# Weight buffers at eight offsets from a multiple of 512 bytes, and each unit's matmuls sorted by width

## The chip, the core and the metric

The kernel runs on one core of a Trainium2 chip. The metric is the device time of one execution in microseconds (us), the median of three runs. TensorE multiplies matrices, VectorE (DVE in the profile) and ScalarE (ACT) work elementwise, GpSimd is POOL, and SyncE (SP) issues most DMAs. A matmul on TensorE has two operands in the on-chip memory SBUF: the stationary one (128 columns of 128 partitions here), which is loaded into the array by an instruction of its own (PEld, LDWEIGHTS in the profile), and the moving one, which is streamed through, up to 512 columns. The result is added up in PSUM.

## What is computed

A decoder trunk of two layers on 256 tokens of width 2048, in float32. Cut to what matters:

```python
for l in range(2):
    h = rms_norm(x, norm_mix[l])
    p = h @ w_in[l]                        # (256, 2048) @ (2048, 6656)
    x = x + mixers(p) @ w_out[l]           # three kinds of attention; (256, 2048) @ (2048, 2048)
    u = rms_norm(x, norm_ffn[l])
    gate = causal_dwconv(u @ w_gate[l])    # (256, 2048) @ (2048, 5504)
    x = x + (silu(gate) * (u @ w_up[l])) @ w_down[l]    # (256, 5504) @ (5504, 2048)
return rms_norm(x)
```

Nearly all work is in these five products with weights.

## The kernel before

**Precision in two parts.** A float32 number is held as a pair of float32r numbers, hi and lo, where lo is what hi leaves over. The product of two such numbers is made of hi·hi, hi·lo and lo·hi. The operand (h, the mixers' output or the activation) lies in tiles `hp`, `mixp` and `actp`, which hold, for 128 rows of the reduction, 256 tokens of hi and then 256 tokens of lo, so 512 columns. A weight tile comes by DMA as float32 (`raw`, five buffers) and is split: ScalarE copies it into `whi` (line 169, by the helper in line 122), VectorE subtracts into `wlo` (line 170).

**Units.** The weights come in units of 128 x 1024 elements, 788 in all. `dma_unit` loads unit u + 7, `split_unit` splits unit u + 3, and `mm_unit` issues the matmuls of unit u; each is called once per step of one loop over all units. `whi` and `wlo` have four buffers each of 4096 bytes in a partition, used in turn. After the matmuls of a unit the loop lets the mixers' and other elementwise steps go on (`steps.run`).

**Two modes.** In mode B (676 units: the projections that are wanted transposed, the output, gate, up and down products) a slice of 128 weight columns is stationary. For each slice there are two matmuls: line 202 with the `whi` slice as stationary operand and all 512 columns of the operand as moving one (hi·hi and lo·hi side by side), and line 203 with the `wlo` slice and the operand's 256 columns of hi. A unit has eight such pairs. The text calls the matmul of 512 columns H and that of 256 L; before, they alternate H, L, H, L. In mode A (112 units) the operand's slices of 128 tokens are stationary and 512 weight columns move, three matmuls (lines 209, 210 and 211) for each slice, 12 in a unit.

**Accumulators.** Each output block (a chunk) adds up in one of two accumulators, `acc`, each of two PSUM banks. When a chunk has had its last matmul, its results are taken over by ScalarE and VectorE while the next chunk fills the other accumulator. The down product has 43 slices of the reduction for a chunk, four in a unit, so some of its units hold the end of one chunk and the start of the next.

**Addresses.** A slice of weights is 512 bytes long in a partition, and the operands' slices start at multiples of 1024 bytes (mode B) or 512 (mode A) in their tiles. In the program as built all these tiles, `whi`, `wlo`, `hp`, `mixp` and `actp`, start 128 bytes behind a multiple of 512, so every weight load and every moving operand of these matmuls starts at the same remainder of 512 bytes.

**Order of the work.** The order on each engine is the order in which the code issues instructions; the tile framework adds the semaphore waits. The first H of a unit waits for ScalarE's copy, the first L for VectorE's subtraction, ScalarE's copy into a `whi` buffer for the last matmul that read it four units ago.

Of the kernel before, what the change touches and what calls it, by code (L numbers as in the profile page):

```python
# [10 lines left out]
F32 = mybir.dt.float32  # L11
F32R = mybir.dt.float32r
# [4 lines left out]
P = 128  # L17
S = 256
# [64 lines left out]
def hybrid_kernel(ctx: ExitStack, tc: tile.TileContext, io):  # L83
    nc = tc.nc

    wpool = ctx.enter_context(tc.tile_pool(name="wpool", bufs=4))
# [33 lines left out]
    def act(out, in_, fn, **kw):  # L120
        want(fn)
        nc.scalar.activation(out, in_, fn, **kw)  # L122
# [30 lines left out]
    def dma_unit(u, parts=1, between=None):  # L153
# [5 lines left out]
                between()  # L159
        raws[u] = t  # L160

    def split_unit(u, parts=1):
        r = raws.pop(u)
        hi = wpool.tile([P, 1024], F32R, name=f"whi{u}", tag="whi")
        lo = wpool.tile([P, 1024], F32R, name=f"wlo{u}", tag="wlo")
        n = 1024 // parts
        for i in range(parts):
            cs = slice(i * n, (i + 1) * n)
            act(hi[:, cs], r[:, cs], AF.Copy)
            nc.vector.tensor_tensor(lo[:, cs], r[:, cs], hi[:, cs].bitcast(F32), op=OP.subtract)  # L170
        splits[u] = (hi, lo)

    def mm_unit(u, f_only=None):
        hi, lo = splits[u]
        ended = []
        off = 0
        for ch, kt in units[u][1]:
            if ch.begin is not None and not ch.begun:
                ch.begin()
            for _ in range(200):  # L180
                if ch.need(kt) and (ch.acc is not None or ACC.free):
                    break
                steps.run(1e9, 1e9)
            assert ch.need(kt)
            if ch.acc is None:
                ch.acc = ACC.get([P, 1024], F32, f"acc_{u}")
            acc = ch.acc[0]
            first = not ch.begun
            ch.begun = True
            last = ch.left == 1  # L190
            if f_only != 0:
                ch.left -= 1
            if u == nu - 1:
                last = kt == NF - 1
            pair, j = ch.operand(kt)
            x = pair[:, j].rearrange("p a t -> p (a t)")
            if ch.mode == "B":
                for f in range(ch.ncol // P) if f_only is None else (f_only,):
                    w = slice(off + f * P, off + (f + 1) * P)
                    o = acc[:, f * 512:(f + 1) * 512]  # L200

                    nc.tensor.matmul(o, hi[:, w], x, start=first, stop=False, skip_group_check=True)  # L202
                    nc.tensor.matmul(o[:, 0:S], lo[:, w], x[:, 0:S], start=False, stop=last, skip_group_check=True)  # L203
            else:
                w = slice(off, off + 512)
                for t in range(2):
                    xh, xl = x[:, t * P:(t + 1) * P], x[:, S + t * P:S + (t + 1) * P]
                    o = acc[:, t * 512:(t + 1) * 512]
                    nc.tensor.matmul(o, xh, hi[:, w], start=first, stop=False)  # L209
                    nc.tensor.matmul(o, xh, lo[:, w], start=False, stop=False)  # L210
                    nc.tensor.matmul(o, xl, hi[:, w], start=False, stop=last)  # L211
            off += ch.ncol
            if ch.left == 0:
                ended.append(ch)
        return ended


# [139 lines left out]
    part = {}  # L357
# [742 lines left out]
    steps.add(first_stats(), 0)  # L1100
    build_h(0, g0)
    split_unit(0, 2)
    dma_unit(3)
    build_h(1, g0)
    split_unit(1)
    dma_unit(4)
    xin(6)
    xin(7)
    build_h(2, g0)
    build_h(3, g0)  # L1110
    split_unit(2)
    dma_unit(5)
    dma_unit(6)
    for u in range(nu):
        if u in (1, 2):
            build_h(2 * u + 2, g0)
            build_h(2 * u + 3, g0)
        if u + 3 < nu:
            split_unit(u + 3)
        if u + 7 < nu:  # L1120
            dma_unit(u + 7)
        if u == nu - 1:

            mm_unit(u, 0)
            ended = mm_unit(u, 1)
        else:
            ended = mm_unit(u)
        del splits[u]
        steps.run(1.25, 1.3)
        for ch in ended:  # L1130
            if ch.after is not None:
                ch.after()
            ch.done(ch.acc)
            new = steps.live[[x[1] for x in steps.live].index(steps.n - 1)]
            try:
                next(new[2])
            except StopIteration:
                steps.live.remove(new)
# [86 lines left out]
```

## Time and profile before

| | |
|---|---|
| median of 3 runs | 2298.92 us (2298.28 to 2299.11) |
| the profiled execution | 2298.39 us |
| its span, first to last instruction | 2296.5 us |
| TensorE busy, matmuls | 2274.6 us (99%), 12724 instructions |
| weight loads busy | 1978.1 us (86%), 12724 instructions |
| VectorE busy | 1512.8 us (66%) |
| ScalarE busy | 1087.1 us (47%) |
| bytes moved by DMA | 425.10 MB, mean 185 GB/s |

The profile records one execution. A row of its groups gives the line, the engine, the operation, the tiles (output <- inputs), shapes, the count, busy time and the mean duration of one, and the idle time of the engine before these instructions with what ended it. A row of the timeline gives start and duration in us, engine, line and operation. TensorE's matmuls are pipelined: the record of one lasts longer than the distance to the start of the next, and the ends are modelled, so this document takes distances from start to start. A matmul of plain float32 is recorded as two, so there are more records than matmuls.

### The profile page before, as it was taken

The page shows a single profiled execution, that of the slowest core. Times are in us where ns is not written, and L with a number is a line of the kernel's source. Part 1 is how long each engine was busy: PE and PEld are TensorE (multiplying, and loading weights), DVE is VectorE, ACT ScalarE, POOL GpSimd, SP SyncE. Part 2 cuts the span into 40 slices and gives each one's busy share as a digit, 9 for nine tenths or more (in the row PEclk, how much of TensorE's full clock was granted, in tenths as well). Part 3 has the DMA queues.
Part 4 walks back from the last instruction along what each step waited for, and adds up shares of the span by engine and source line. Part 5 has one row for each costly group of instructions (what it writes and reads, how often), then busy time and mean ns, then how long its engine had stood idle before and what let it go on. Part 6 is the DMA issues. An engine that isn't in the chain of part 4 may idle for free.

```text
span 2296.5 us, 32374 instructions
## 1 busy us (share of the span) xinstructions
PE 2274.6 (99%) x12724; PEld 1978.1 (86%) x12724; DVE 1512.8 (66%) x1898; ACT 1087.1 (47%) x1388; POOL 176.9 (8%) x150
## 2 busy tenths in 40 slices
PE   8999999999999999999999999999999999999997
PEld 7788888888888888888888888888888888888886
DVE  5685556777777777555567755577777777765554
ACT  5654544454444444444456454444444444444442
POOL 0150001100000000000012400020000000001111
PEclk9999999999999999999999999999999999999999
DMA  7454454655555555555555445555555555555553
GB/s 264 167 173 168 165 189 167 197 186 193 188 190 191 193 189 187 192 190 188 191 195 181 165 166 173 175 179 198 193 189 187 193 192 186 191 192 188 189 192 110
DMA packets 120580, 425.10 MB, mean 185 GB/s; under 512 B 13515, under 2 KB 17132, under 8 KB 120428
## 3 DMA queue, kind: packets, MB, share of 16 engines
q1 hardware_dynamic: 118412, 420.50, 53.3%
q10 hardware_dynamic: 2016, 2.54, 0.3%
q8 instruction: 100, 1.64, 0.3%
q14 instruction: 52, 0.43, 0.1%
HBM read 419.31 MB, written 3.67 MB: 184 GB/s over the span
## 4 chain that ended last, share of the span: by engine, by line
PE 94%; POOL 2%; issue 1%; DVE 1%; ACT 1%; DMA 0%; DVEq 0%; SPq 0%; ACTq 0%; POOLq 0%
PE acc L202 54%; PE acc L203 28%; PE acc L209 3%; PE acc L211 3%; PE acc L210 3%; POOL hx L488 0%; POOL hx L489 0%; DVE wlo L170 0%; DMA raw<-in_w_b 0%; PE ps_rstd L1096 0%; PE ps_qk L680 0%; PE ps_o L710 0%; ACT whi L122 0%; PE ps_pt L700 0%; PE ps_rs L793 0%
## 5 line engine op out<-in xcount | busy, mean ns | idle before, releaser
L170 DVE TENSOR_TENSOR wlo<-raw,whi 128x1024 fp32r<-128x1024 f32 (+1 forms) x789 | 998.9, 1269 | 728.0 <-ACT whi L122 721.5
L202 PE MATMUL acc<-hp,whi 128*128 128x512 f32 x3520 | 1230.1, 394 | 6.7 <-ACT whi L122 5.8
L122 ACT ACTIVATE whi<-raw 128x1024 fp32r<-128x1024 f32 (+1 forms) x789 | 831.5, 1056 | 809.6 <-PE acc L202 553.5
L203 PE MATMUL acc<-hp,wlo 128*128 128x256 f32 x3520 | 986.1, 280 | 0.0
L202 PEld LDWEIGHTS acc<-hp,whi 128*128 128x128 f32 x3520 | 660.3, 188 | 154.9 <-ACT whi L122 5.8
L203 PEld LDWEIGHTS acc<-hp,wlo 128*128 128x128 f32 x3520 | 666.8, 189 | 0.7 <-DVE wlo L170 0.4
L202 PE MATMUL acc<-actp,whi 128*128 128x512 f32 x1376 | 477.1, 391 | 0.0
L203 PE MATMUL acc<-actp,wlo 128*128 128x256 f32 x1376 | 385.3, 280 | 0.0
L202 PEld LDWEIGHTS acc<-actp,whi 128*128 128x128 f32 x1376 | 257.4, 187 | 56.3
L203 PEld LDWEIGHTS acc<-actp,wlo 128*128 128x128 f32 x1376 | 260.4, 189 | 0.0
L209 PE MATMUL acc<-whi,hp 128*128 128x512 f32 x448 | 181.6, 405 | 0.0
L202 PE MATMUL acc<-mixp,whi 128*128 128x512 f32 x512 | 178.9, 395 | 0.0
L248 POOL TENSOR_TENSOR sq<-xt 128x512 f32<-128x512 f32 x31 | 33.2, 1070 | 1862.1 <-DVE xt L319 1198.7
L211 PE MATMUL acc<-whi,hp 128*128 128x512 f32 x448 | 175.1, 391 | 0.0
L210 PE MATMUL acc<-wlo,hp 128*128 128x512 f32 x448 | 174.6, 390 | 0.0
L203 PE MATMUL acc<-mixp,wlo 128*128 128x256 f32 x512 | 142.0, 277 | 0.0
L202 PEld LDWEIGHTS acc<-mixp,whi 128*128 128x128 f32 x512 | 96.1, 188 | 21.9
L209 PEld LDWEIGHTS acc<-whi,hp 128*128 128x128 f32 x448 | 84.2, 188 | 18.8 <-issue 1.6
L211 PEld LDWEIGHTS acc<-whi,hp 128*128 128x128 f32 x448 | 84.1, 188 | 18.2
L210 PEld LDWEIGHTS acc<-wlo,hp 128*128 128x128 f32 x448 | 84.3, 188 | 16.5
L203 PEld LDWEIGHTS acc<-mixp,wlo 128*128 128x128 f32 x512 | 96.2, 188 | 0.0
L122 ACT ACTIVATE actp<-up 128x512 fp32r<-128x512 f32 (+1 forms) x44 | 27.4, 623 | 83.3 <-DVE up L849 83.3
(196 smaller groups left out, 1189.8 us busy)
## 6 DMA issues: line engine op xcount, KB each, us to landing
raw<-in_w_d SPq DMA_DIRECT2D x172, 512.0 KB, 3.3
raw<-in_w_g SPq DMA_DIRECT2D x168, 512.0 KB, 3.2
raw<-in_w_u SPq DMA_DIRECT2D x168, 512.0 KB, 3.2
raw<-in_w_a SPq DMA_DIRECT2D x112, 512.0 KB, 3.2
raw<-in_w_b SPq DMA_DIRECT2D x95, 512.0 KB, 3.2
raw<-in_w_out SPq DMA_DIRECT2D x64, 512.0 KB, 3.3
xt<-in_x SPq DMA_DIRECT2D x8, 256.0 KB, 6.1
bias<-brow_d SPq DMA_DIRECT2D x4, 512.0 KB, 5.1
```

The lines of the kernel that those rows point to most:

```text
L122: nc.scalar.activation(out, in_, fn, **kw)
L170: nc.vector.tensor_tensor(lo[:, cs], r[:, cs], hi[:, cs].bitcast(F32), op=OP.subtract)
L202: nc.tensor.matmul(o, hi[:, w], x, start=first, stop=False, skip_group_check=True)
L203: nc.tensor.matmul(o[:, 0:S], lo[:, w], x[:, 0:S], start=False, stop=last, skip_group_check=True)
L209: nc.tensor.matmul(o, xh, hi[:, w], start=first, stop=False)
L210: nc.tensor.matmul(o, xh, lo[:, w], start=False, stop=False)
L211: nc.tensor.matmul(o, xl, hi[:, w], start=False, stop=last)
L248: nc.gpsimd.tensor_tensor(sq, x, x, op=OP.mult)
```

## The change

**Pads.** The four rotating buffers of `whi` and `wlo` become eight single buffers, named by the unit number modulo 4, and ahead of each, when it is first made, a small tile is allocated that is never used: 32 bytes ahead of `whi0`, 96 ahead of `wlo0`, 64 ahead of each other one. The buffers then start 32, 128, 192, 256, 320, 384, 448 and 512 bytes further on than the operands do, counted in remainders of 512: in this order `whi0`, `wlo0`, `whi1`, `wlo1`, `whi2`, `wlo2`, `whi3`, `wlo3`. The last of them has the operands' own remainder again. The operand tiles keep theirs. A buffer is still used by every fourth unit.

**Order.** `mm_unit` first collects the pieces of the unit, then issues all H, then all L. Mode A keeps its order.

```diff
+    lead = {"whi0": 32, "wlo0": 96, "whi1": 64, "wlo1": 64, "whi2": 64, "wlo2": 64, "whi3": 64, "wlo3": 64}
+
+    def split_tile(kind, u):
+        tag = f"{kind}{u % 4}"
+        if tag in lead:
+            wpool.tile([P, lead.pop(tag) // 4], F32, name=f"lead_{tag}", tag=f"lead_{tag}", bufs=1)
+        return wpool.tile([P, 1024], F32R, name=f"{kind}{u}", tag=tag, bufs=1)
...
-        hi = wpool.tile([P, 1024], F32R, name=f"whi{u}", tag="whi")
-        lo = wpool.tile([P, 1024], F32R, name=f"wlo{u}", tag="wlo")
+        hi = split_tile("whi", u)
+        lo = split_tile("wlo", u)
...
+            pieces.append((ch, pair[:, j].rearrange("p a t -> p (a t)"), ch.acc[0], off, first, last))
...
+        for part in range(2):
+            for ch, x, acc, off, first, last in pieces:
+                if ch.mode == "A":
+                    continue
                 for f in range(ch.ncol // P) if f_only is None else (f_only,):
                     w = slice(off + f * P, off + (f + 1) * P)
                     o = acc[:, f * 512:(f + 1) * 512]
 
-                    nc.tensor.matmul(o, hi[:, w], x, start=first, stop=False, skip_group_check=True)
-                    nc.tensor.matmul(o[:, 0:S], lo[:, w], x[:, 0:S], start=False, stop=last, skip_group_check=True)
...
+                    if part == 0:
+                        nc.tensor.matmul(o, hi[:, w], x, start=first, stop=False, skip_group_check=True)
+                    else:
+                        nc.tensor.matmul(o[:, 0:S], lo[:, w], x[:, 0:S], start=False, stop=last, skip_group_check=True)
```

TensorE's rows in the gate product of layer 0, unit 160 and the start of unit 161, before (the tiles' numbers tell buffers apart; each H and L shown here stands four times in a row, in turns, and the repeats are left out):

```order
L202 MATMUL acc_160_4406<-hp_3163,whi160_4324 128x512
L203 MATMUL acc_160_4406<-hp_3163,wlo160_4325 128x256
...
L202 MATMUL acc_160_4406<-hp_3196,whi160_4324 128x512
L203 MATMUL acc_160_4406<-hp_3196,wlo160_4325 128x256
...
L202 MATMUL acc_160_4406<-hp_3296,whi161_4347 128x512
L203 MATMUL acc_160_4406<-hp_3296,wlo161_4348 128x256
```

And the same units in the changed kernel:

```order
L221 MATMUL acc_160_4414<-hp_3171,whi160_4332 128x512 x4
L221 MATMUL acc_160_4414<-hp_3204,whi160_4332 128x512 x4
L223 MATMUL acc_160_4414<-hp_3171,wlo160_4333 128x256 x4
L223 MATMUL acc_160_4414<-hp_3204,wlo160_4333 128x256 x4
L221 MATMUL acc_160_4414<-hp_3304,whi161_4355 128x512 x4
L221 MATMUL acc_160_4414<-hp_3404,whi161_4355 128x512 x4
```

Where there were eight changes from 512 to 256 columns in a unit there is one, between its eighth and ninth matmul.

In the down product of layer 0, TensorE's rows where unit 318 holds the end of one chunk and the start of the next, before:

```order
L202 MATMUL acc_308_8054<-actp_8123,whi318_8214 128x512
L203 MATMUL acc_308_8054<-actp_8123,wlo318_8215 128x256
...
L202 MATMUL acc_318_8298<-actp_4077,whi318_8214 128x512
L203 MATMUL acc_318_8298<-actp_4077,wlo318_8215 128x256
...
L202 MATMUL acc_318_8298<-actp_4077,whi319_8236 128x512
```

And after:

```order
L221 MATMUL acc_308_8062<-actp_8131,whi318_8222 128x512 x2
L221 MATMUL acc_318_8294<-actp_4085,whi318_8222 128x512 x2
L223 MATMUL acc_308_8062<-actp_8027,wlo318_8223 128x256 x4
L223 MATMUL acc_308_8062<-actp_8131,wlo318_8223 128x256 x2
L223 MATMUL acc_318_8294<-actp_4085,wlo318_8223 128x256 x2
L221 MATMUL acc_318_8294<-actp_4085,whi319_8244 128x512 x2
```

The old chunk's last L now stands behind the new chunk's first two H.

More of the change, by code (lines that the diff above doesn't have):

```diff
@@ L176, in mm_unit @@
         off = 0
+        pieces = []
         for ch, kt in units[u][1]:
@@ L186, in mm_unit @@
                 ch.acc = ACC.get([P, 1024], F32, f"acc_{u}")
-            acc = ch.acc[0]
             first = not ch.begun
@@ L195, in mm_unit @@
             pair, j = ch.operand(kt)
-            x = pair[:, j].rearrange("p a t -> p (a t)")
-            if ch.mode == "B":
+            pieces.append((ch, pair[:, j].rearrange("p a t -> p (a t)"), ch.acc[0], off, first, last))
+            off += ch.ncol
+            if ch.left == 0:
+                ended.append(ch)
+        for part in range(2):
+            for ch, x, acc, off, first, last in pieces:
+                if ch.mode == "A":
+                    continue
                 for f in range(ch.ncol // P) if f_only is None else (f_only,):
@@ L200, in mm_unit @@
                     o = acc[:, f * 512:(f + 1) * 512]
[L202 to L214, printed above, removed]
+                    if part == 0:
+                        nc.tensor.matmul(o, hi[:, w], x, start=first, stop=False, skip_group_check=True)
+                    else:
+                        nc.tensor.matmul(o[:, 0:S], lo[:, w], x[:, 0:S], start=False, stop=last, skip_group_check=True)
+        for ch, x, acc, off, first, last in pieces:
+            if ch.mode == "B":
+                continue
+            w = slice(off, off + 512)
+            for t in range(2):
+                xh, xl = x[:, t * P:(t + 1) * P], x[:, S + t * P:S + (t + 1) * P]
+                o = acc[:, t * 512:(t + 1) * 512]
+                nc.tensor.matmul(o, xh, hi[:, w], start=first, stop=False)
+                nc.tensor.matmul(o, xh, lo[:, w], start=False, stop=False)
+                nc.tensor.matmul(o, xl, hi[:, w], start=False, stop=last)
         return ended
```

## Prediction

> **What bounds the kernel now.** I read the page first: engine shares, TensorE's clock, then the chain of work that ended last.
>
> ```profile
> span 2296.5 us, 32374 instructions
> PE 2274.6 (99%) x12724; PEld 1978.1 (86%) x12724; DVE 1512.8 (66%) x1898; ACT 1087.1 (47%) x1388; POOL 176.9 (8%) x150
> PEclk9999999999999999999999999999999999999999
> PE 94%; POOL 2%; issue 1%; DVE 1%; ACT 1%; DMA 0%; DVEq 0%; SPq 0%; ACTq 0%; POOLq 0%
> ```
>
> TensorE is busy for 99% of the span at the full granted clock, and 94% of the chain is TensorE. The groups of instructions say which matmuls these are (the last two columns are the idle time before them and its cause).
>
> ```profile
> L202 PE MATMUL acc<-hp,whi 128*128 128x512 f32 x3520 | 1230.1, 394 | 6.7 <-ACT whi L122 5.8
> L202 PE MATMUL acc<-actp,whi 128*128 128x512 f32 x1376 | 477.1, 391 | 0.0
> L202 PE MATMUL acc<-mixp,whi 128*128 128x512 f32 x512 | 178.9, 395 | 0.0
> L209 PE MATMUL acc<-whi,hp 128*128 128x512 f32 x448 | 181.6, 405 | 0.0
> L211 PE MATMUL acc<-whi,hp 128*128 128x512 f32 x448 | 175.1, 391 | 0.0
> L210 PE MATMUL acc<-wlo,hp 128*128 128x512 f32 x448 | 174.6, 390 | 0.0
> L203 PEld LDWEIGHTS acc<-hp,wlo 128*128 128x128 f32 x3520 | 666.8, 189 | 0.7 <-DVE wlo L170 0.4
> ```
>
> So there are 3520 + 1376 + 512 = 5408 pairs of mode B (one matmul of 512 columns, H, and one of 256, L) and 3 x 448 = 1344 matmuls of mode A (512 columns): 12160 in all, each with its own weight load, and almost no idle time. A mean of 394 ns is no price, since neighbours overlap; the price is the distance from start to start. I take it from stretches where nothing else runs on TensorE: from the stages view for mode B in the feed-forward part of layer 0 (first row: window, busy, matmuls in brackets), and from the timeline for mode A, the first and the last start of 48 matmuls (four units of 12).
>
> ```profile
> 500.00:850.00 350.00, 350.00 (x2021) 1.00 0.55 190
> ```
>
> ```profile
> 1184.35 0.39 PE L209 MATMUL acc<-whi,hp 128*128 128x512 f32 x1
> 1195.23 0.39 PE L209 MATMUL acc<-whi,hp 128*128 128x512 f32 x1
> ```
>
> A pair costs 350 us / 1010.5 = 346.4 ns, a matmul of mode A 10.88 us / 48 = 226.7 ns. If a matmul costs r per column and b besides, 512r + b = 226.7 and 768r + 2b = 346.4 give r = 0.42 ns and b = about 13 ns. The streaming cannot be changed by this edit. The 13 ns can, in principle: 12160 x 13 ns = 158 us of the span.
>
> What are these 13 ns? Two places of the timeline tell something. The first is the start of the kernel, where TensorE runs at half its pace (the clock column says 1.00 there too, so the profile doesn't show why):
>
> ```profile
> 7.56 0.63 PE L202 MATMUL acc<-hp,whi 128*128 128x512 f32 x1
> 8.20 0.63 PE L202 MATMUL acc<-hp,whi 128*128 128x512 f32 x1
> ```
>
> A pair takes 640 ns there, which is 768 columns at 0.83 ns, exactly twice r, and nothing besides. So the extra is no fixed toll for each matmul: it appears only when the moving operand is read at full pace, as if the weight load that runs beside it took turns of the same read. The second place is in layer 1, in units of mode B behind a run of mode A; the rows are the start of an H and the start of the next A, seven units or 56 pairs later.
>
> ```profile
> 1200.76 0.40 PE L202 MATMUL acc<-hp,whi 128*128 128x512 f32 x1
> 1220.55 0.40 PE L209 MATMUL acc<-whi,hp 128*128 128x512 f32 x1
> ```
>
> These pairs cost 19.79 us / 56 = 353.4 ns with the same tiles at the same remainders of 512 bytes: 7.0 ns more than in the feed-forward part. So the extra depends on how loads and streams stand to each other in time, and it settles into one of two states.
>
> **The change part by part.** *The pads.* Seven of eight weight buffers get another remainder of 512 bytes against the operand tiles. Their price is not in the trace of before, because there all weights and operands have the same remainder. From both sides: if the remainder shifts loads against streams as favourably as possible, it could take off all of the 13 ns; the nearest row for an unfavourable shift is the 7.0 ns a pair (3.5 ns a matmul) of the state above. I take nothing, because the trace has met several relations in time already (the start of every stage, every interruption by another matmul) and always came back to 346.4 or 353.4 ns, never to less: an offset in address looks to me like another start of the same game. The Trainium skill (SBUF — State Buffer, Who interferes with whom) says that TensorE reads through two independent ports, one for moving data and one for weights, and waits on no engine; by that the pads are worth nothing. The trace doesn't agree on the reason, since a load beside a stream does cost it 13 ns here.
>
> *The order inside a unit.* H and L each keep their count, columns, weight load and accumulator. If every matmul kept its own share, a unit would cost what it did, 8 x 346.4 ns. What is new is that each of the 676 units of mode B (5408 / 8) now has a run of eight H, then a run of eight L, and so two changes of kind. Before, such changes only stand at stage borders. From B to A (the L is followed by 512-column matmuls) the timeline has, for the first A, the one eight later and the one twelve after that:
>
> ```profile
> 320.30 0.39 PE L209 MATMUL acc<-whi,hp 128*128 128x512 f32 x1
> 322.14 0.39 PE L211 MATMUL acc<-whi,hp 128*128 128x512 f32 x1
> 324.86 0.39 PE L211 MATMUL acc<-whi,hp 128*128 128x512 f32 x1
> ```
>
> The first eight take 1.84 us, 27 ns above 8 x 226.7; the next twelve take 2.72 us, 226.7 each. A run of 512-column matmuls behind a 256-column one needs about eight to settle, which is as long as the new run is. From A to B the first pair is:
>
> ```profile
> 1197.95 0.39 PE L202 MATMUL acc<-hp,whi 128*128 128x512 f32 x1
> 1198.29 0.40 PE L202 MATMUL acc<-hp,whi 128*128 128x512 f32 x1
> ```
>
> 340 ns, so some 6 to 7 ns come back there. Net 20 ns for each unit: 676 x 20 ns = 13.5 us. L behind L has no row (no 256-column matmul of this dtype stands behind another); its bounds are the cheapest and dearest shares seen, 0 and 27 ns more for a unit if it needs settling as well, and a gain isn't excluded but I have no row for one. I take 0.
>
> *Waits.* The page's waits, in total, times and longest:
>
> ```profile
> DVE wlo L170 <- ACT whi L122: 721.5, 633, 4.8
> ACT whi L122 <- PE acc L202: 553.5, 329, 2.4
> ACT up L122 <- PE acc L203: 76.8, 42, 1.8
> ```
>
> The hi buffer is now read last in the middle of its unit, so ScalarE's copy may start up to eight L earlier (half of 8 x 346 ns at most); the lo buffer is needed seven H later (7 x 227 ns = 1.6 us). Both only lengthen waits of engines at 66% and 47%. Where a unit of the down projection holds the end of one accumulator and the start of the next, the ended one now waits for up to six more H (1.4 us); the other accumulator is in use for another 43 x 2 pairs (30 us), which covers it. At the start:
>
> ```profile
> 5.82 0.80 PE L202 MATMUL acc<-hp,whi 128*128 128x512 f32 x1 [5.82 <-ACT whi L122]
> 6.54 0.58 PE L203 MATMUL acc<-hp,wlo 128*128 128x256 f32 x1
> ```
>
> The first L follows the first H after 0.72 us, of which some tenths may be spared when other H stand between them. The slow state of the 56 pairs, 0.39 us there, could go as well. All of this I set to 0, with 1 us of gain as the bound.
>
> **The sum.** The profiled execution took 2298.39 us (its span of 2296.5 and 1.9 around it), 0.5 us under the median of the three runs, 2298.92. 2298.4 + 13.5 = 2311.9; with the half us, 2312.
>
> **Rivals.** *Nothing moves* (2299, 2294 to 2303): runs of eight settle into the same 13 ns a matmul, since nearly all stages of before did so whatever came ahead, and the pads do nothing. Against it: the 27 ns at 320 us, which recurs at the other borders.
>
> *The pads keep loads and streams apart (faster).* Place: every weight load beside a full-pace stream. For it: at half pace the cost is nil, so it is a collision, and the 353.4 against 346.4 ns shows that it depends on a relation between the two reads. All 12160 matmuls of before have one relation of addresses, so the trace can't say that another is no better. Price: one step like that between the two states, 3.5 ns for a matmul, on seven buffers of eight: 12160 x 7/8 x 3.5 ns = 37 us, so 2262; all 13 ns would give 2160. It decides from 13.5 us / 12160 = 1.1 ns a matmul upwards, where it outweighs the changes of kind. The Trainium skill (TensorE: Matmul & The Clock Gate, Back-to-back issue gap) gives columns / 2.4 GHz + 2.5 ns for a warm matmul; an estimate from it is 215.8 ns for 512 columns where the trace has 226.7, so by that page some 11 ns of each matmul would be there to win.
>
> *The pads make it worse*: other remainders hold the stream in the dearer state, +3.5 ns on seven of eight: 37 us, 2336. For it: the state exists; against it: only 56 pairs in a row and some shorter pieces were in it.
>
> **How the numbers follow.** Changes of kind cost (the forecast; its own range goes from half the price, 2306, to twice, 2326) 0.34; nothing moves 0.28; faster by the pads 0.29; slower by the pads 0.09. A measurement of this kernel can tell about 0.2%, 4.6 us, from no change. Faster: 0.29 and 0.01 of the case at rest, 0.30; within 0.2%: 0.27; slower: 0.34 + 0.09 = 0.43. The range goes from 2240, which takes in a gain by the pads of one and a half steps (56 us) and leaves out larger ones, some 0.10, to 2336, which leaves out about 0.05.
>
> **What would show it.** In the feed-forward stage after, an H run's distances start above 227 ns and fall, and eight pairs of a unit take 2.79 us instead of 2.77. If distances differ between the four hi buffers (unit number modulo 4), the pads matter; if all H take 227 ns and all L 120 ns, nothing moved. I am wrong if a unit takes 2.77 us or less, or if mode A, whose order is kept, leaves 226.7 ns: that would be the pads alone.

## The result and the profile after

| | before | after |
|---|---|---|
| median, measured side by side | 2298.74 us (4 runs) | 2317.22 us (4 runs, 2317.03 to 2317.41) |
| ratio, 95% interval | | 1.0078 [1.0065, 1.0091] |
| span of the profiled execution | 2296.5 us | 2315.2 us |

The change makes the kernel 18.5 us slower. The forecast was 2312 us, slower, inside a range of 2240 to 2336. The page of the changed kernel, the same four lines that were shown of before:

```profile
span 2315.2 us, 32374 instructions
PE 2294.0 (99%) x12724; PEld 1984.8 (86%) x12724; DVE 1495.9 (65%) x1898; ACT 1084.4 (47%) x1388; POOL 181.3 (8%) x150
PEclk9999999999999999999999999999999999999998
PE 94%; POOL 2%; issue 1%; DVE 1%; ACT 1%; DMA 0%; SPq 0%; DVEq 0%; ACTq 0%; POOLq 0%
```

Counts, clock and chain are as before; TensorE's busy time has grown by 19.4 us, the span by 18.7. So the time was not lost to a wait: the same matmuls cost more. Where, a unit at a time, is read from the timeline. These are the first H of five units in a row in the feed-forward part of layer 0 (start, duration of the whole run of eight), with one run of L between:

```profile
619.58 2.02 PE L221 MATMUL acc<-hp,whi 128*128 128x512 f32 x8
621.43 1.10 PE L223 MATMUL acc<-hp,wlo 128*128 128x256 f32 x8
622.38 2.00 PE L221 MATMUL acc<-hp,whi 128*128 128x512 f32 x8
...
625.16 2.03 PE L221 MATMUL acc<-hp,whi 128*128 128x512 f32 x8
...
627.98 2.00 PE L221 MATMUL acc<-hp,whi 128*128 128x512 f32 x8
...
630.77 0.40 PE L221 MATMUL acc<-hp,whi 128*128 128x512 f32 x1
```

From start to start the four units take 2.80, 2.78, 2.82 and 2.79 us. The same distances over the whole stage, unit number modulo 4 from 0 to 3, are 2796, 2783, 2820 and 2794 ns. Before, every one was 2773; there the starts of two units, four apart, are

```profile
615.51 0.39 PE L202 MATMUL acc<-hp,whi 128*128 128x512 f32 x1
...
626.61 0.39 PE L202 MATMUL acc<-hp,whi 128*128 128x512 f32 x1
```

So units have grown, and the four buffers differ. The second place to look is mode A, whose order is the same. The first matmul of a unit in layer 1, and of the one four units on:

```profile
1190.82 0.39 PE L231 MATMUL acc<-whi,hp 128*128 128x512 f32 x1
...
1201.93 0.39 PE L231 MATMUL acc<-whi,hp 128*128 128x512 f32 x1
```

11.11 us, where it was 10.88: 231.5 ns a matmul instead of 226.7. The order of these matmuls is the same, so this points at the pads; e1, which has the order alone, shows it.

The one wait that the change was to shorten did get shorter: what ScalarE's copy into `whi` waits for TensorE has gone from 553.5 to 461.0 us, since H now come first and let go of the buffer sooner.

```profile
ACT whi L122 <- PE acc L221: 461.0, 284, 1.8
```

It is worth nothing here, since ScalarE is busy for 47% of the span and TensorE doesn't wait for it.

I summed the 787 distances from the start of one unit to the start of the next in each trace and took before's away: mode B +15.3 us, mode A +3.8 us. Two theories stood against each other for these: that the changes of kind cost 13.5 us as forecast and the pads the rest, or that the pads do all or most of it.

### The profile page after: what moved, and what is told of

The parts are those of the page before. It is cut to its first block, busy times and chain, and to the rows that moved or that the text cites. A ratio compares the mean times of both kernels' runs of the same rounds, so it can differ in the third digit from the quotient of the medians.

```text
span 2315.2 us, 32374 instructions
## 1 busy us (share of the span) xinstructions
PE 2294.0 (99%) x12724; PEld 1984.8 (86%) x12724; DVE 1495.9 (65%) x1898; ACT 1084.4 (47%) x1388; POOL 181.3 (8%) x150
## 4 chain that ended last, share of the span: by engine, by line
PE 94%; POOL 2%; issue 1%; DVE 1%; ACT 1%; DMA 0%; SPq 0%; DVEq 0%; ACTq 0%; POOLq 0%
PE acc L221 54%; PE acc L223 28%; PE acc L231 3%; PE acc L232 3%; PE acc L233 3%; POOL hx L507 0%; POOL hx L508 0%; DVE wlo L180 0%; DMA raw<-in_w_b 0%; PE ps_rstd L1115 0%; PE ps_qk L699 0%; PE ps_o L729 0%; ACT whi L122 0%; PE ps_pt L719 0%; PE ps_rs L812 0%
## 5 line engine op out<-in xcount | busy, mean ns | idle before, releaser
L122 ACT ACTIVATE whi<-raw 128x1024 fp32r<-128x1024 f32 (+1 forms) x789 | 830.0, 1056 | 709.3 <-PE acc L221 461.0
L221 PE MATMUL acc<-hp,whi 128*128 128x512 f32 x3520 | 891.5, 395 | 6.2 <-DVE hp L253 6.1
L221 PEld LDWEIGHTS acc<-hp,whi 128*128 128x128 f32 x3520 | 632.5, 189 | 125.2 <-ACT whi L122 6.4
L223 PEld LDWEIGHTS acc<-hp,wlo 128*128 128x128 f32 x3520 | 480.1, 189 | 37.5
L223 PE MATMUL acc<-hp,wlo 128*128 128x256 f32 x3520 | 490.0, 282 | 0.0
L221 PE MATMUL acc<-actp,whi 128*128 128x512 f32 x1376 | 346.2, 393 | 0.0
L223 PEld LDWEIGHTS acc<-actp,wlo 128*128 128x128 f32 x1376 | 187.5, 189 | 14.7
L223 PE MATMUL acc<-actp,wlo 128*128 128x256 f32 x1376 | 191.4, 282 | 0.0
L221 PE MATMUL acc<-mixp,whi 128*128 128x512 f32 x512 | 129.7, 395 | 0.0
L223 PEld LDWEIGHTS acc<-mixp,wlo 128*128 128x128 f32 x512 | 69.7, 189 | 5.5
L122 ACT ACTIVATE hp<-xt,par 128x256 fp32r<-128x256 f32 x64 | 28.7, 500 | 94.6 <-DVE xt L338 93.2
```

## The experiments

A number of bytes below is the offset of a buffer against the operand tiles, counted in remainders of 512, as in the section on the change. "Unit" is the distance from the start of one unit of mode B to the next in the feed-forward part of layer 0, before 2773 ns; its columns alone are 8 x 320 = 2560 ns, by the 640 ns of a pair at half pace. So the extra of a unit of before is 213 ns.

The extra isn't made by the other engines. Near the end of before, in units 785 and 786, all weights are loaded and split, and VectorE, ScalarE and GpSimd are idle and the DMA nearly so (the columns are the window, then busy time and instructions of PE, PEld, DVE, ACT and POOL, the clock, and the DMA's share and rate):

```profile
2272.60:2278.10 5.50, 5.50 (x34) 4.84 (x33) 0.00 (x0) 0.00 (x0) 0.00 (x0) 1.00 0.01 3
```

These two units take 2773 and 2774 ns, like those of the feed-forward stage. So TensorE's own loads and streams are enough to make the extra.

### The two halves of the change

**e1: the order alone.** The buffers stay as they were.

```diff
+        for part in range(2):
+            for ch, x, acc, off, first, last in pieces:
...
+                    if part == 0:
+                        nc.tensor.matmul(o, hi[:, w], x, start=first, stop=False, skip_group_check=True)
+                    else:
+                        nc.tensor.matmul(o[:, 0:S], lo[:, w], x[:, 0:S], start=False, stop=last, skip_group_check=True)
```

> The sorted order without the pads (weight buffers as before, four of each, all at the operands' remainder of 512 bytes). Theory K (the changes of kind cost, as predicted): mode B units take about 2.80 us as in the changed kernel (2774 + 25 ns), mode A units go back to 2720 ns, in all about 2311 us (676 x 25 ns = 16.9 us less what little the order saves elsewhere). Theory P (the pads cost, the order nothing): 2774 ns a unit, 2297 to 2300 us. If both have a part, a unit of mode B lies between 2774 and 2799 ns.

2310.43 us, ratio 1.005 [1.0035, 1.0065], +11.8 us. The timeline's rows of one unit and the start of the unit four later:

```profile
617.89 2.00 PE L213 MATMUL acc<-hp,whi 128*128 128x512 f32 x8
619.74 1.12 PE L215 MATMUL acc<-hp,wlo 128*128 128x256 f32 x8
620.69 2.00 PE L213 MATMUL acc<-hp,whi 128*128 128x512 f32 x8
...
629.07 0.40 PE L213 MATMUL acc<-hp,whi 128*128 128x512 f32 x1
```

Four units take 11.18 us, so 2.795 us each; the median over the stage is 2793 ns, 20 ns over before. The eight H take 1.85 us where eight settled ones take 8 x 226.7 = 1.81. From start to start, in single matmuls, their extra over the bare columns is 20, 22, 15, 19, 18, 13, 13 and 13 ns: a run of H settles after five. The first L has 7 ns, each later one 12 or 13. These are the +27 and the -7 ns of the sum. Mode A stays:

```profile
1188.05 0.39 PE L223 MATMUL acc<-whi,hp 128*128 128x512 f32 x1
...
1198.93 0.39 PE L223 MATMUL acc<-whi,hp 128*128 128x512 f32 x1
```

That is 10.88 us for four units, as before. So the time and the price of a unit are what the first theory (K) gave, 2311 us.

**e2: the pads alone.** H and L alternate as before.

```diff
+    lead = {"whi0": 32, "wlo0": 96, "whi1": 64, "wlo1": 64, "whi2": 64, "wlo2": 64, "whi3": 64, "wlo3": 64}
...
-        hi = wpool.tile([P, 1024], F32R, name=f"whi{u}", tag="whi")
+        hi = split_tile("whi", u)
```

> The eight pads with the order of before (H, L, H, L). Theory K: pairs stay at 346.7 ns, a unit of mode B at 2774 ns; only mode A's units, which rose from 2720 to about 2775 ns in the changed kernel though their order is kept, stay dear: 112 x 55 ns = 6 us, so about 2305 us. Theory P: the units of mode B differ by buffer (unit number modulo 4) and cost about 2.80 us on the mean, so about 2317 us.

2306.05 us, ratio 1.0032 [1.002, 1.0043], +7.4 us. Five starts of units in a row:

```profile
619.77 0.40 PE L210 MATMUL acc<-hp,whi 128*128 128x512 f32 x1
...
622.60 0.40 PE L210 MATMUL acc<-hp,whi 128*128 128x512 f32 x1
...
625.35 0.40 PE L210 MATMUL acc<-hp,whi 128*128 128x512 f32 x1
...
628.15 0.39 PE L210 MATMUL acc<-hp,whi 128*128 128x512 f32 x1
...
630.89 0.40 PE L210 MATMUL acc<-hp,whi 128*128 128x512 f32 x1
```

2.83, 2.75, 2.80 and 2.74 us: over the stage 2837, 2747, 2802 and 2735 ns, so +64, -26, +29 and -38 against before. The four buffers do four things, two of them gains, and the mean hides them. Mode A grows as well, by 50, 82, 52 and 50 ns in those units of layer 1 that run without interruption, and by 3.9 us over all its units. Mode B grows by 5.6 us in this trace, but 2.1 us of that stand in the kernel's first eight units: the profiled execution took 2307.79 us, 1.7 above the median, so about 3.5 us are mode B's part of the 7.4. The time lies near the 2305 us that K expected, but not for K's reason: K had mode B's units unchanged at 2774 ns. The two halves add up to 11.8 + 7.4 = 19.2 us, beside 18.5 together.

### What an order costs

**e3 and e4: groups of two and of four.** Buffers as before; in a unit two H, two L and so on (e3, shown), or four and four (e4, with 4 for each 2).

```diff
+        for g in range(0, len(pairs), 2):
+            for o, w, x, first, last in pairs[g:g + 2]:
+                nc.tensor.matmul(o, hi[:, w], x, start=first, stop=False, skip_group_check=True)
+            for o, w, x, first, last in pairs[g:g + 2]:
+                nc.tensor.matmul(o[:, 0:S], lo[:, w], x[:, 0:S], start=False, stop=last, skip_group_check=True)
```

> No pads; a unit's pairs in groups of two: H H L L, four times. Theory K: four times as many runs as with eight, each too short to settle; if a change costs 25 ns whatever the run's length, 100 ns a unit and 2366 us; if only matmuls not yet settled cost, not less than the sorted order's 2311 us. Theory P: 2774 ns a unit, 2297 to 2300 us.

> No pads; groups of four: H x4, L x4, twice in a unit. Theory K: between the groups of two and the runs of eight, 2311 to 2332 us. Theory P: 2774 ns a unit, 2297 to 2300 us.

e3: 2307.88 us, ratio 1.0038 [1.0023, 1.0053]; four units:

```profile
618.47 0.63 PE L212 MATMUL acc<-hp,whi 128*128 128x512 f32 x2
...
629.62 0.40 PE L212 MATMUL acc<-hp,whi 128*128 128x512 f32 x1
```

e4: 2316.94 us, ratio 1.0077 [1.0062, 1.0092]:

```profile
620.19 1.09 PE L212 MATMUL acc<-hp,whi 128*128 128x512 f32 x4
...
631.39 0.39 PE L212 MATMUL acc<-hp,whi 128*128 128x512 f32 x1
```

Over the stage, units take 2787 and 2800 ns. So runs of 1, 2, 4 and 8 cost 0, 13, 27 and 20 ns a unit, with eight, four, two and one change from H to L. The cost is neither so much for a change nor less with fewer changes; e3 came out below both times that K gave (2366, or not less than 2311 us) and above P's 2300. Nor do the unsettled matmuls of e1 carry over: if each run began with e1's extras, runs of two and four would cost some 35 and 32 ns a unit. What sets the price of a run isn't shown.

### What an address costs

The next kernels lay the eight buffers out by a table: pads in bytes ahead of each, in the order of allocation. H and L alternate unless it is said.

**e5: four places for hi.** lo at 0; `whi0` to `whi3` at 96, 128, 160 and 224.

```diff
+    place = [('wlo0', 0), ('wlo1', 0), ('wlo2', 0), ('wlo3', 0), ('whi0', 96), ('whi1', 32), ('whi2', 32), ('whi3', 64), ('tail', 288)]
```

> Order of before (H, L, H, L). All lo buffers at the operands' remainder, the hi buffers of units 0, 1, 2, 3 modulo 4 at 96, 128, 160 and 224 bytes beyond it, to see which remainders of the hi part are cheap. With pads alone a unit cost 2735 ns where hi stood at 448 and lo at 0, and 2747 ns at 192 and 256. Theory P (the remainder of hi against the operand decides, with a period of 256 bytes): units at 160 and 224, next to 192, are below 2774 ns, those at 96 and 128 at or above it. Rival Q (the four units' effects pass from one to the next, a cheap unit is only cheap behind a dear one): no unit falls below 2774 ns by more than a few ns on the mean of the four.

2312.62 us in one run.

```profile
618.73 0.40 PE L219 MATMUL acc<-hp,whi 128*128 128x512 f32 x1
...
621.53 0.39 PE L219 MATMUL acc<-hp,whi 128*128 128x512 f32 x1
...
624.35 0.39 PE L219 MATMUL acc<-hp,whi 128*128 128x512 f32 x1
...
627.14 0.39 PE L219 MATMUL acc<-hp,whi 128*128 128x512 f32 x1
...
629.89 0.40 PE L219 MATMUL acc<-hp,whi 128*128 128x512 f32 x1
```

The distances are 2804, 2817, 2789 and 2756 ns over the stage: three of the four places are dearer than 0, one is cheaper. The miss at 160 counts against the simple rule that was expected (P). Q expected no gain on the mean of the four, and their mean is 2792 ns.

**e6: four places for lo.** hi at 192, lo at 224, 288, 320 and 448.

```diff
+    place = [('whi0', 192), ('whi1', 0), ('whi2', 0), ('whi3', 0), ('wlo0', 32), ('wlo1', 64), ('wlo2', 32), ('wlo3', 128), ('tail', 64)]
```

> Order of before. All hi buffers 192 bytes beyond the operands' remainder, the lo buffers of units 0, 1, 2, 3 modulo 4 at 224, 288, 320 and 448 beyond it. Theory P: lo is cheap at 0 and 256 only (2735 and 2747 ns a unit with pads alone) and dear at 128 and 384 (2837 and 2802), so 224 and 288, next to 256, lie between these, 320 and 448 above 2774 ns. Rival Q: no order by remainder.

2315.62 us in one run; units of 2787, 2787, 2775 and 2831 ns, none cheaper than before. They lie in the wide ranges that P gave, but 320, further from 256, is cheaper than 224 and 288, against P's order. The place of lo matters as well, and hi at 192 is no help by itself.

**e7: lo at 0, hi at 192.** The four `whi` are at 192 or 448 (192 and half of 512 more). In mode A, where the weights are the moving operand, hi is written 64 bytes further on, which brings it to 0 or 256.

```diff
+    place = [('wlo0', 0), ('wlo1', 0), ('wlo2', 0), ('wlo3', 0), ('whi0', 192), ('whi1', 192), ('whi2', 192), ('whi3', 192)]
+        cols = 1040 if kind == "whi" else 1024
+        hi = hi[:, 16:1040] if units[u][1][0][0].mode == "A" else hi[:, 0:1024]
```

> Order of before. Lo buffers at the operands' remainder, all four hi buffers 192 or 448 bytes beyond it for mode B; in mode A hi is written 64 bytes further on in the same buffer, so at 0 or 256. Theory P: all units of mode B take 2735 to 2747 ns, 26 to 38 ns less than before: 676 x 38 = 26 us, 2273 to 2281 us; mode A stays at 2720 ns. Rival Q: 2297 to 2302 us.

2263.16 us, ratio 0.9846 [0.983, 0.9863], 35.5 us faster than before and the fastest kernel of the study. The page, the stages view of the same 350 us as in the prediction, and the timeline's first and fifth start of a unit:

```profile
span 2261.3 us, 32374 instructions
PE 2238.5 (99%) x12724; PEld 1955.3 (86%) x12724; DVE 1512.4 (67%) x1898; ACT 1086.3 (48%) x1388; POOL 177.7 (8%) x150
```

```profile
500.00:850.00 350.00, 350.00 (x2061) 1.00 0.59 194
```

```profile
608.66 0.39 PE L220 MATMUL acc<-hp,whi 128*128 128x512 f32 x1
...
619.54 0.39 PE L220 MATMUL acc<-hp,whi 128*128 128x512 f32 x1
```

Four units take 10.88 us, 2720 ns each and the same in all four buffers: a pair of 340 ns instead of 346.4, an extra of 160 ns a unit instead of 213. The instructions and their order on TensorE are before's; only addresses differ. Mode B gains 35.0 us over all units, mode A, whose weights lie at 0 or 256 there, nothing. That is 10 us more than the best that P expected (2273 us): P took 2735 to 2747 ns from e2's cheap units, whose first pairs, behind a neighbour at other places, are dearer. From their fourth pair to their seventh e2's trace has 340 ns a pair too. In units 785 and 786 of e7, where the other engines are idle again, a unit takes 2720 ns as well, so the gain doesn't come from the other engines either.

**e8: half the stationary columns.** Buffers and order of before. Except in the first and last slice of a chunk each matmul of mode B loads 64 weight columns instead of 128, so half the output rows lack those products; columns streamed are the same.

```diff
+                        nc.tensor.matmul(o[0:64], hi[:, w.start:w.start + 64], x, start=False, stop=False, skip_group_check=True)
...
+                        nc.tensor.matmul(o[0:64, 0:S], lo[:, w.start:w.start + 64], x[:, 0:S], start=False, stop=False, skip_group_check=True)
```

> Order and buffers of before, but in mode B all matmuls except those of a chunk's first and last slice load 64 weight columns instead of 128 and give 64 of the 128 output rows; half of the products of these rows are left out. The streams keep 512 and 256 columns. Theory C (the 13 ns are the weight load's reads that meet the stream's): about half the extra goes, 6 to 7 ns on some 9700 matmuls, 60 to 70 us: 2230 to 2240 us. Rival F (a toll for every matmul at full pace, whatever it loads): 2297 to 2301 us.

2265.35 us, ratio 0.9856 [0.9841, 0.9871], 33.4 us less. The loads' group, and the starts of two units, four apart:

```profile
L209 PEld LDWEIGHTS acc<-hp,wlo 128*64 128x64 f32 x3080 | 413.4, 134 | 0.5
```

```profile
608.60 0.40 PE L203 MATMUL acc<-hp,whi 128*128 128x512 f32 x1
...
619.51 0.40 PE L203 MATMUL acc<-hp,whi 128*128 128x512 f32 x1
```

A load's record shrinks from 189 to 134 ns and the extra of a unit from 213 to 160 ns; units that begin or end a chunk, and so hold full loads, have 173. Half the columns take away a quarter of the extra, not half, so the time lies between the two that were expected (C with 2230 to 2240, F with 2297 to 2301 us): the extra is neither a toll that nothing changes nor proportional to the columns loaded. These matmuls also write half the output rows, so this run alone doesn't tell the shorter load from the smaller output; e7, in which only addresses change, speaks for the load.

### Both together

**e9: e7's places, sorted order.** The table is e7's, the loop e1's.

> The kernel with hi at 192 or 448 and lo at 0 (2263 us in the order H, L, H, L), now with the sorted order: all H of a unit, then all L. Theory K (a change of kind costs the same, whatever the remainders): 2720 + 20 ns a unit, 2276 us. Rival R (the favourable remainders work through the alternation: H is read beside a load at 0, L beside one at 192; sorted, H is read beside loads at 192): the gain is lost and the sorting paid besides, as in the changed kernel's units at 192 and 256 (2783 ns): 2300 to 2312 us.

2305.68 us, ratio 1.003 [1.0019, 1.0041].

```profile
618.20 2.01 PE L229 MATMUL acc<-hp,whi 128*128 128x512 f32 x8
...
629.35 0.40 PE L229 MATMUL acc<-hp,whi 128*128 128x512 f32 x1
```

Units of 2787 ns: e7's gain is gone, and sorting costs 67 ns a unit at these places where it cost 20 at equal remainders. The expectation that the gain would outlive the sorting (2276 us) failed. The time is in rival R's range; R's reason, the remainder of the load beside each stream, is put to the test again in e11.

**e10: a fine scan around 192.** lo at 0, hi at 176, 208, 200 and 184 (the second and fourth and half of 512 more).

```diff
+    place = [('wlo0', 0), ('wlo1', 0), ('wlo2', 0), ('wlo3', 0), ('whi0', 160), ('whi1', 224), ('whi2', 192), ('whi3', 160), ('tail', 32)]
+        at = (4, 4, 2, 6)[u % 4]
+        hi = hi[:, at:at + 1024]
```

> Order H, L, H, L, lo at the operands' remainder, hi of units 0, 1, 2, 3 modulo 4 at 176, 208 (464), 200 and 184 (440) bytes beyond it, in steps below 32 bytes. Theory P with 32 bytes as the step that counts: 200 and 208 behave like 192 (2720 ns a unit, or near it with such neighbours), 176 and 184 like 160 (2789 ns). With a finer step: something between, or even below 2720 ns.

2314.85 us in one run; units of 2826, 2773, 2772 and 2789 ns. The unit at 200 begins here, and the next one here:

```profile
626.91 0.39 PE L221 MATMUL acc<-hp,whi 128*128 128x512 f32 x1
...
629.68 0.39 PE L221 MATMUL acc<-hp,whi 128*128 128x512 f32 x1
```

Its eight pairs take 346 to 347 ns each, from the first to the last, so this isn't a neighbour's doing. A place 8 bytes beside 192 has lost the whole gain, so no step of 32 bytes or more describes it.

**e11 and e12: the mirror image.** hi at 0, lo at 192 or 448 (in mode A 0 or 256), sorted in e11, alternating in e12.

```diff
+    place = [('whi0', 0), ('whi1', 0), ('whi2', 0), ('whi3', 0), ('wlo0', 192), ('wlo1', 192), ('wlo2', 192), ('wlo3', 192)]
+        lo = lo[:, 16:1040] if units[u][1][0][0].mode == "A" else lo[:, 0:1024]
```

> Sorted order with the roles of the remainders exchanged: hi at the operands' remainder, lo 192 or 448 bytes beyond it (mode A reads lo 64 bytes further on, at 0 or 256). Sorted, an H stands beside the load of the next hi slice and an L beside that of the next lo slice, so here H stands beside loads at 0 and L beside loads at 192, as in the alternating kernel of 2263 us. Theory S (what counts is the remainder of the load beside the stream and the stream's width): the L run gets cheaper, about 16 cycles or 6.7 ns an L, 50 ns a unit: 2793 - 50 = 2743 ns, about 2276 us. Rival T (it is the alternation itself that settles so low): 2787 ns or more a unit, 2305 us and up.

> Order H, L, H, L with the exchanged remainders: hi at 0, lo at 192 or 448. Now H stands beside loads at 192, L beside loads at 0. Theory S: none of the gain of the 2263 us kernel; a unit at or above 2774 ns, 2299 us or slower. Rival T (any difference of 192 between hi and lo will do when the two alternate): 2720 ns, 2263 us.

e11: 2319.28 us, ratio 1.0086 [1.0071, 1.0101], and e12: 2311.82 us, ratio 1.0054 [1.0037, 1.0071]. Four units in each:

```profile
618.06 2.03 PE L229 MATMUL acc<-hp,whi 128*128 128x512 f32 x8
...
629.31 0.40 PE L229 MATMUL acc<-hp,whi 128*128 128x512 f32 x1
```

```profile
616.88 0.40 PE L220 MATMUL acc<-hp,whi 128*128 128x512 f32 x1
...
628.08 0.40 PE L220 MATMUL acc<-hp,whi 128*128 128x512 f32 x1
```

From these come units of 2813 and 2800 ns. Of the two theories that these runs were to tell apart, as the expectations name them, S is right for the alternating kernel and falls for the sorted one, T the other way round. Neither explains both. In all three pairs (before and e1, e7 and e9, e12 and e11) the sorted order is dearer, by 20, 67 and 13 ns a unit: what an order costs depends on the addresses.

## Why the prediction was right

**What bounds the kernel** held: TensorE's matmuls at 99% of the span, one behind the other, and a price of columns plus an extra that depends on the load beside the stream. e7 and e8 show that the extra is no fixed toll: 213 ns a unit go down to 160 when addresses change, or when loads of half the columns write half the rows. The Trainium skill (SBUF — State Buffer, Who interferes with whom) says that TensorE's two read ports are independent; by that alone the place of a weight buffer would cost nothing, but in these traces it moves a pair between 340 ns (e7) and 355 ns (e2's first buffer, 2837 / 8).

**Changes of kind, 676 x 20 ns = 13.5 us,** were right in mechanism and size. e1 has 20 ns a unit, made of the two terms that were read from before's borders between modes. Over all units of its trace it is 12.3 us. Of these 11.5 stand in the 579 units from the output product of each layer on, which is the full 20 ns each, and the rest at the kernel's start and in the projections. There before had units in the dearer state, twelve of them without interruption (2810 to 2831 ns), and these take 2765 to 2794 ns when sorted. Against 20 ns more each that is 0.7 us, the gain that was named and set to 0 with 1 us as its bound. The reading that about eight H are needed to settle was cautious: it takes five. And the 27 ns don't stand at every border of before from B to A, as the prediction has it: three of the eight have 38, and a wait covers the first. In e1 it is 27.

**The pads, taken as 0,** is the term that was mis-sized: +7.4 us alone (e2), and in the change as made 18.5 - 11.8 = 6.7 us. The prediction had named the sign of it: it would be wrong if mode A left 226.7 ns, and mode A went to 231.5 (11.11 us / 48). So the forecast of 13.5 us covers the order's part of the 18.5 and no more; no case on the prediction's list had both the order and the pads cost. The step that failed reads "an offset in address looks to me like another start of the same game". It isn't: with the buffers at other remainders the units have other prices and keep them, unit after unit, for each buffer its own. "Never to less" than 346.4 ns was true of before's trace and no bound: e7 has 340 ns. The trace of before held one relation of addresses only, as the second rival said, and nothing that was read from it could price another. That the term comes out small is luck of this one table: its four buffers moved a unit by +64, -26, +29 and -38 ns.

**The waits, taken as 0,** were right: TensorE's busy share and the chain are the same, and the 92 us that ScalarE's copy no longer waits are worth nothing. (The prediction says that both moves only lengthen waits; ScalarE's became shorter.)

**The rivals.** Nothing moves: out, by e1 and by mode A. The pads as a gain: wrong for this table, but right that another layout can be cheaper, and close in price: e7 is 35.5 us below before where the rival said 37, by 3.3 ns a matmul (53 ns / 16) on the 10816 of mode B where the rival had 3.5 on seven eighths of all 12160. That the totals agree so well is in part chance, since the matmuls counted aren't the same. The pads as a loss of 37 us: the sign was right, the size a fifth of it, because buffers of both signs lie side by side.

**What stays open** is which reads meet. The measured units, lo at 0 and alternating, are 2773 ns for hi at 0, 2804 at 96, 2817 at 128, 2789 at 160, 2826 at 176, 2720 at 192, 2772 at 200 and 2756 at 224; neither S nor T gives these and e11 and e12 as well. In the scans with four places the neighbours differ too, and a unit's first load runs beside its neighbour's last stream, so each of these numbers may be some ns off. The operand tiles kept their remainder in every run. So it isn't shown whether the distance between the two addresses counts or the place of the weight buffer by itself; a run with operands and weights moved together would tell. Whether another pair of places beats 2720 ns wasn't tried.

## What to carry to other kernels

Where weight loads run beside streams back to back, the places of the weight buffers within 512 bytes are a knob of some 2% (2263 to 2316 us here for the same instructions in the same order, e7 and e6); the trace of one layout can't price another, so try several layouts, one for all buffers at a time, and read each buffer's price from start to start. A layout and an order have to be tried together: the best layout that was tried for alternating widths lost its gain when the widths were sorted. And a price that is paid while a run settles can be read from borders which the kernel has already: the 20 ns from before's borders between modes came back as 20 ns a unit in the feed-forward units of e1, at the same layout. At other layouts sorting cost 67 and 13.

## What was not expected of the hardware

- An offset of 8 bytes decides: hi at 192 gives 2720 ns a unit, hi at 200 gives 2772 (lo at 0, H and L alternating).
- The mean price of a run doesn't go with its length: runs of 1, 2, 4 and 8 cost 346.6, 348.4, 350.0 and 349.1 ns a pair.
- Mode A, with no change of its order, pays 32 to 106 ns more a unit of 12 matmuls when the weights, its moving operand, lie at the other remainders that were tried, and nothing when they lie at 0 or 256 (e7, e11 and e12: 2720 ns).
